# Attention heads of a gated-linear-attention layer cut into fifteen placed pieces

## The chip, the cores and the metric

The kernel runs on one core of a Trainium2 chip. The metric is the device time of one execution in microseconds (us). Engines are named as in the profile: PE is TensorE's matmul, PEld its weight load, DVE VectorE, ACT ScalarE, POOL GpSimd, SP the queue from which every DMA of this kernel is issued.

## The reference, cut to what matters

One decoder layer over 2048 tokens of width 1024: a gated-linear-attention mixer, then a gated feed-forward part with a causal convolution, each modulated by a conditioning vector, each with a layer normalisation after it.

```python
def gla_mixer(h, w_in, w_a2, b_a, norm_g, w_o):       # 4 heads, key width 128, value width 256, chunks of 64
    q, k, v, r, a_lr = jnp.split(h @ w_in, [...], axis=-1)
    log_a = jax.nn.log_sigmoid((a_lr @ w_a2 + b_a)) / 16.0
    bcum = jnp.cumsum(chunks(log_a, GLA_DK), axis=3)
    q_dec, k_inv, k_dec = qf * exp(bcum), kf * exp(-bcum), kf * exp(blast - bcum)
    att = where(causal, q_dec @ k_inv.T, 0);  o_intra = att @ vf
    def step(state, xs):                               # over the chunks
        o = q_dec @ state
        state = state * exp(blast)[..., None] + k_dec.T @ v
    o = (o_intra + o_inter) * rsqrt(mean(o * o) + 1e-5) * norm_g
    return (o * silu(r)) @ w_o

def conv_ffn(h, w_up, conv_w, conv_b, w_down): ...     # (silu(conv(u)) * g) @ w_down

x = layer_norm(alpha * x + (1 + gate) * mixer(x * (1 + scale) + shift))   # and the same with conv_ffn
```

## The kernel before

Every float32 product is made of three float32r products: an operand is split into a high half (a cast on ACT, L105) and a low half (a subtraction on DVE, L108), and `mm3` issues high x high, high x low, low x high (L111 to L113).

The tokens are four blocks (`tb` 0 to 3) of 512. First come the projections of block 0 and of `v` and `r` for all blocks, the latter by seven products for a 2x2 block product (`v_group`, `r_group`). Four products `X[0]`, `X[4]`, `X[2]`, `X[1]` of operands also serve the rank-16 gate rows: block 1's first half is `X[0]` plus the difference `X[4]`, so `gate_rows` multiplies both with `waw` and adds them in PSUM. `decays` makes the decay factors of a head from such rows: a product, then ACT and DVE in turn (L582 to L597).

Then comes the attention stage, in *units*. It goes through seven segments, `Q1 Q2 O0 Q3 O1 O2 O3`: a Q segment makes queries and keys of a block, an O segment multiplies a block's gated heads with `w_o`. A segment has eight units of 24 matmuls of 128x512 into four banks `ps_mm`; after four units the banks are emptied (`qk_out` by ACT, L667 and L668; `zs`, the residual sum, by DVE, L1375). `tick()` between units calls what a table puts there. `at_unit(u, fn)` enters a step; in the version before, a step's place is rounded down to a whole unit.

A head is a chain of such steps, `head_l` (loads of `E` and `qk`), `head_s` (decayed queries `Q`, keys `KI` and `KK`, on DVE), `head_a` (transposes of `KK`, L1208, and two groups of scores `Q,KI`, masked into `attm`, L1223 and L1224), `head_v` and `head_r` (loads), `head_b` (products `v,KTt` that update the state `S`, L1254, whose split halves `Shl` are made at once), `head_c` (outputs `v,at` and `Shl,Q`, copied to `on`, L1276) and `head_d` (two transposes of `on`, L1290, gated into `sr`, L1292). All of these and the transposes of the normalised rows (`ln1_out`, L1327) use four small banks `ps_w` in turn. `H_AT`, `STEP`, `LN_AT` and the other tables hold the places.

What the tables give is the order in which the code is recorded. A scheduler then orders each engine's instructions by priority and estimated readiness; `tc.high_priority(offset=...)` moves a few forward. All DMAs are issued by SP in one order, and each engine executes its instructions in its order. Weights and operands arrive in four buffers `raw`, and the split halves of two units are made ahead.

```python
STEP = (-1, 0, 2, 2, 3, 4, 5, 7)   # units after H_AT: head_l, _s, _a, _v, _b, _r, _c, _d
```

Of the kernel before, what the change touches and what calls it, by code (L numbers as in the profile page):

```python
# [17 lines left out]
P = 128  # L18
D = 1024
S = 2048  # L20
# [19 lines left out]
def kernel(  # L40
# [164 lines left out]
    a3_d = [dram.tile([96, TB], F32, name=f"a3_d{t}") for t in range(NTB)]  # L205
    xm1_d = [[dram.tile([P, 1024], F32, name=f"xm1_d{t}_{r}") for r in range(4)] for t in range(NTB)]
# [174 lines left out]
    def at_unit(u, fn, *a):  # L381
        steps.setdefault(math.floor(u), []).append((u, fn, a))

    def tick():
        u = pos[0]
        pos[0] += 1
        for _, fn, a in sorted(steps.pop(u, []), key=lambda s: s[0]):
            fn(*a)
# [39 lines left out]
    if True:  # L428
# [139 lines left out]
        def decays(tb, heads):  # L568
# [7 lines left out]
            for h in heads:  # L576
# [26 lines left out]
        def mm_a(pa, w, xs, kts):  # L603
            for kt in kts:
                for n, xm in enumerate(xs[kt]):
                    end = kt == KT - 1 and n == len(xs[kt]) - 1
                    nc.tensor.matmul(pa[0:96], w[:, kt], xm[0], start=kt == 0 and n == 0, stop=False)
                    nc.tensor.matmul(pa[0:96], w[:, kt], xm[1], start=False, stop=end)
# [7 lines left out]

        def waw_load():
# [22 lines left out]
        def s_part(banks, u, xm, lo_last=False):  # L640
# [9 lines left out]
            for n in range(4):  # L650
                for k in range(2):
                    kt = 2 * u + k
                    mm3(banks[n], (wv[:, 0, n, k], wv[:, 1, n, k]), xm[kt],
                        kt == 0, kt == KT - 1)

# [8 lines left out]
        def qk_out(tb, h, pq, pk):  # L664
            t = raw_tile("qk")
            with tc.high_priority(offset=0):
                nc.scalar.copy(t[:, 0:512], pq)  # L667
                nc.scalar.copy(t[:, 512:1024], pk)  # L668
            store(qk_d[tb][h], t)
            made.add(("qk", tb, h))  # L670
# [4 lines left out]
        def gemm_start():  # L675
# [51 lines left out]
            for pr in range(4):  # L727
# [35 lines left out]
                mm_a(pa, waw, {kt: [xm[kt]] for kt in kts}, kts)  # L763
# [10 lines left out]
            evac_a(pa, 0)  # L774
# [67 lines left out]
        def v_group(hf, X):  # L842
# [7 lines left out]
            for i in PROD:  # L850
# [22 lines left out]
                for t in range(4):  # L873
                    if i in (0, 5, 6):
                        dst = {0: p1, 5: u2, 6: u3}[i][t]
                        with tc.high_priority(offset=600):
                            nc.scalar.copy(dst, A[t])
# [184 lines left out]
        R_AT = ((8, 11, 12), (43, 45, 46))  # L1062
# [3 lines left out]
        WAW_AT = (11, 44, 52)  # L1066
        for u in WAW_AT:
            at_unit(u, waw_load)
        GR_AT = (17, 49, 56)
# [12 lines left out]
        M_AT = (36, 37.5, 38, 39, 40, 41, 42, 43, 51, 52, 53, 54, 55, 56, 57, 58)  # L1082
        MF_AT = (50, 49, 56, 61)
# [4 lines left out]
        at_unit(63, mod2)  # L1088
        at_unit(GR_AT[1], gate_rows, 2, XN1)
        at_unit(GR_AT[2], gate_rows, 3, XN1)  # L1090
        G_AT = (54, 55, 56, 57, 58, 59, 60, 61, 62)
# [54 lines left out]
        assert pos[0] == B0, pos  # L1146
        evx.close()
# [8 lines left out]
        Shl = [None] * NH  # L1156
# [37 lines left out]
        def head_v(H):  # L1194
            H["v"] = []
            for s in range(4):
                v = ab.tile([P, 2, DV], F32R, tag="v", name="v", bufs=7)
# [7 lines left out]
        def head_a(H):  # L1205
# [3 lines left out]
            KTt = zp.tile([P, 2, 512], F32R, tag="z", name="KTt")  # L1209
            with tc.high_priority(offset=60):  # L1210
                split(KTt[:, 0], KTt[:, 1], pt)
            H["KT"] = KTt
            KI, Q = H["KI"], H["Q"]
            H["at"] = []
            for g in range(2):
                pa = psum("w", 4)
                pav = pa[:, 0:384].rearrange("p (s c) -> p s c", s=2)
                for i in range(2):
                    s = 2 * g + i
                    tk = slice(s * P, s * P + P)  # L1220
                    mm3(pav[:, i], (KI[:, 0, tk], KI[:, 1, tk]), (Q[:, 0, s], Q[:, 1, s]), True, True)
                am = attm[g]
# [3 lines left out]
                at = ab.tile([P, 2, 2, P], F32R, tag="at", name="at", bufs=4)  # L1226
                split(at[:, 0], at[:, 1], am)
                H["at"].append(at)

        def head_b(H):  # L1230
            h, v, KTt, el = H["h"], H["v"], H["KT"], H["el"]
            H["S"] = []
            for g in range(2):
                pst = psum("w", 4)
                for i in range(2):
                    s = 2 * g + i
                    H["S"].append(Shl[h])
                    if H["last"] and s == 3:
                        continue
                    tk = slice(s * P, s * P + P)  # L1240
                    po = pst[:, i * DV:i * DV + DV]
                    mm3(po, (KTt[:, 0, tk], KTt[:, 1, tk]), (v[s][:, 0], v[s][:, 1]), True, True)
                for i in range(2):
                    s = 2 * g + i
                    if H["last"] and s == 3:
                        continue
                    po = pst[:, i * DV:i * DV + DV]
                    old = S32[:, h] if i == 0 else new
                    new = S32[:, h] if i == 1 else t2p.tile([P, DV], F32, tag="t2", name="S1")
                    with tc.high_priority(offset=0):  # L1250
                        if H["S"][s] is None:
                            nc.vector.tensor_copy(new, po)
                        else:
                            nc.vector.scalar_tensor_tensor(new, old, el[:, 1, s:s + 1], po, op0=ALU.mult, op1=ALU.add)  # L1254
                    st1 = ab.tile([P, 2, DV], F32R, tag="Shl", name="Shl", bufs=8)
                    split(st1[:, 0], st1[:, 1], new)
                    Shl[h] = st1
                    if i == 0:
                        H["S"][-1] = st1

        def head_c(H):
            h, v, Q = H["h"], H["v"], H["Q"]
            on = zp.tile([P, 4, DV], F32, tag="z", name="on")
            ss = smp.tile([P, 4], F32, tag="ss", name="ss")
            for g in range(2):
                po = psum("w", 4)
                at = H["at"][g]
                for i in range(2):
                    s = 2 * g + i
                    pos_ = po[:, i * DV:i * DV + DV]  # L1270
                    st = H["S"][s]
                    mm3(pos_, (at[:, 0, i], at[:, 1, i]), (v[s][:, 0], v[s][:, 1]), True, st is None)
                    if st is not None:
                        mm3(pos_, (Q[:, 0, s, 0:128], Q[:, 1, s, 0:128]), (st[:, 0], st[:, 1]), False, True)
                with tc.high_priority(offset=0):
                    nc.scalar.copy(on[:, 2 * g:2 * g + 2].rearrange("p s c -> p (s c)"), po)  # L1276
# [6 lines left out]
            H["on"] = on  # L1283

        def head_d(H):
            on, sr = H["on"], H["sr"]
            for e in range(2):
                pt = psum("w", 4)
                for s in range(4):
                    nc.tensor.transpose(pt[:, s * P:s * P + P], on[:, s, e * P:e * P + P], ident)  # L1290
                with tc.high_priority(offset=1200):
                    nc.vector.scalar_tensor_tensor(sr[:, e], pt, ng_sb[:, e:e + 1], sr[:, e], op0=ALU.mult, op1=ALU.mult)  # L1292
# [22 lines left out]

        def ln1_out(tb, zs, prs, by_act=False):
            for pr in prs:
                if zs is None:
                    z = z_tile("zc")
                    for t in range(4):  # L1320
                        load(z[:, t * 256:t * 256 + 256], zn_d[tb * 4 + t][:, pr * 256:pr * 256 + 256])
                for k in range(2):
                    kt = 2 * pr + k
                    pt = psum("w", 4)
                    for t in range(4):
                        src = z[:, t * 256 + k * P:t * 256 + k * P + P] if zs is None else zs[t][:, kt * P:kt * P + P]
                        nc.tensor.transpose(pt[:, t * P:t * P + P], src, ident)  # L1327
                    xt = t2p.tile([P, TB], F32, tag="t2", name="xt")
                    if by_act:
                        nc.scalar.activation(xt, pt, AF.Identity, bias=B2[:, kt:kt + 1], scale=A2[:, kt:kt + 1])  # L1330
                    else:
                        nc.vector.tensor_scalar(xt, pt, A2[:, kt:kt + 1], B2[:, kt:kt + 1], op0=ALU.mult, op1=ALU.add)
# [562 lines left out]
```

## Time and profile before

| | |
|---|---|
| median of 3 runs | 2153.97 us (2152.64 to 2156.61) |
| profiled execution, its own time | 2154.09 us |
| its span, first to last instruction | 2151.4 us |
| PE, DVE, ACT, POOL busy | 2103.0, 1565.6, 1042.9, 109.6 us |
| mean granted clock | 0.992 |

A row of the timeline has the start in us, the duration, engine, line, operation, output and inputs by the program's names, the shape, and in brackets how long the engine stood before it and who released it. Matmuls are pipelined: the duration of one is longer than the distance between two starts.

### The profile page before, as it was taken

How to read it: one execution, taken by the hardware profiler on the slowest of the kernel's cores; microseconds unless marked ns; L12 is line 12 of the kernel's file. 1: busy time of each engine (PE TensorE's matmuls, PEld its weight loads, DVE VectorE, ACT ScalarE, POOL GpSimd, SP SyncE). 2: the span in 40 equal slices, each digit the busy share in tenths (PEclk: the TensorE clock that was granted, in tenths of full speed). 3: DMA queues.
4: the chain of work that ended last, by engine and by line, in shares of the span. 5: the costliest groups of instructions: out<-in, count | busy, mean ns of one | idle time of the engine just before them, and what ended most of it. 6: DMA issues, size and time to landing. Idle time of an engine off the chain costs nothing.

```text
span 2151.4 us, 27162 instructions
## 1 busy us (share of the span) xinstructions
PE 2103.0 (98%) x9741; PEld 1747.5 (81%) x9741; DVE 1565.6 (73%) x2143; ACT 1042.9 (48%) x1523; POOL 109.6 (5%) x250
## 2 busy tenths in 40 slices
PE   9999999999989989999999999999999999999998
PEld 8887788788878868788888888888888888888887
DVE  6856767677876865987878788766666797578557
ACT  4648746665566643554444444333333443344332
POOL 0000000001020111000000000000000000021001
PEclk9999999999999999999999999999999999999999
DMA  9777988878958877677946669877777797677662
GB/s 366 278 262 290 316 293 308 306 275 287 323 198 310 311 277 289 242 271 269 327 175 216 211 231 327 309 253 266 262 255 268 273 334 273 193 239 253 195 204 89
DMA packets 199063, 571.52 MB, mean 266 GB/s; under 512 B 25008, under 2 KB 41776, under 8 KB 189200
## 3 DMA queue, kind: packets, MB, share of 16 engines
q1 hardware_dynamic: 198928, 569.80, 75.1%
q8 instruction: 76, 1.25, 0.2%
q14 instruction: 59, 0.48, 0.1%
HBM read 379.01 MB, written 190.71 MB: 265 GB/s over the span
## 4 chain that ended last, share of the span: by engine, by line
PE 82%; DVE 5%; DMA 5%; ACT 5%; issue 2%; POOL 1%; SPq 0%; DVEq 0%; ACTq 0%; POOLq 0%
PE ps_mm L111 18%; PE ps_mm L113 18%; PE ps_mm L112 18%; PE ps_w L111 8%; PE ps_w L112 8%; PE ps_w L113 8%; DMA raw<-in_wab_dram 1%; ACT hl L105 1%; DMA mraw<-in_mws_dram 1%; PE ps_mm L491 1%; PE ps_w L750 1%; PE ps_w L1327 1%; DVE xc L108 1%; DMA qk<-qk_d 1%; DMA v<-v_d 0%
## 5 line engine op out<-in xcount | busy, mean ns | idle before, releaser
L111 PE MATMUL ps_mm<-xc,hl 128*128 128x512 f32 x856 | 335.7, 392 | 6.0 <-ACT u L422 4.3
L112 PE MATMUL ps_mm<-xc,hl 128*128 128x512 f32 x856 | 334.0, 390 | 0.0
L113 PE MATMUL ps_mm<-xc,hl 128*128 128x512 f32 x856 | 333.2, 390 | 0.1
L111 PEld LDWEIGHTS ps_mm<-xc,hl 128*128 128x128 f32 x856 | 161.1, 188 | 42.0 <-ACT u L422 5.7
L113 PEld LDWEIGHTS ps_mm<-xc,hl 128*128 128x128 f32 x856 | 161.0, 188 | 34.2 <-DVE hl L108 0.7
L112 PEld LDWEIGHTS ps_mm<-xc,hl 128*128 128x128 f32 x856 | 161.2, 188 | 33.6 <-issue 0.5
L111 PE MATMUL ps_w<-xc,hl 128*128 128x512 f32 x432 | 168.4, 390 | 1.1 <-ACT hl L105 1.0
L113 PE MATMUL ps_w<-xc,hl 128*128 128x512 f32 x432 | 168.2, 389 | 0.3 <-DVE hl L108 0.3
L112 PE MATMUL ps_w<-xc,hl 128*128 128x512 f32 x432 | 168.1, 389 | 0.0
L1492 DVE SCALAR_TENSOR_TENSOR ct<-U,cw_sb,ct 128x512 f32<-128x512 f32 x176 | 131.8, 749 | 25.1 <-ACT ct L1486 22.6
L105 ACT CAST dhl<-raw 128x1024 fp32r<-128x1024 f32 x57 | 60.0, 1053 | 159.9 <-PE ps_mm L113 96.7
L422 ACT COPY u<-ps_mm 128x512 f32<-128x512 f32 x104 | 60.8, 584 | 158.2 <-PE ps_mm L113 153.4
L105 ACT CAST hl<-raw 128x1024 fp32r<-128x1024 f32 (+1 forms) x87 | 85.2, 981 | 102.8 <-PE ps_mm L113 39.8
L108 DVE TENSOR_TENSOR hl<-raw,hl 128x1024 fp32r<-128x1024 f32 (+1 forms) x87 | 98.6, 1136 | 49.9 <-ACT hl L105 49.4
L105 ACT CAST hl<-wu 128x1024 fp32r<-128x1024 f32 x82 | 86.3, 1053 | 94.6 <-PE ps_mm L113 68.0
L108 DVE TENSOR_TENSOR hl<-wu,hl 128x1024 fp32r<-128x1024 f32 x82 | 100.3, 1223 | 32.1 <-ACT hl L105 31.5
L108 DVE TENSOR_TENSOR dhl<-raw,dhl 128x1024 fp32r<-128x1024 f32 x57 | 69.7, 1223 | 66.5 <-ACT dhl L105 66.5
L111 PE MATMUL ps_mm<-hl,xg 128*128 128x512 f32 x256 | 102.8, 402 | 6.3 <-DVE zs L1375 4.2
L111 PE MATMUL ps_mm<-dhl 128*128 128x512 f32 x264 | 102.7, 389 | 0.0
L112 PE MATMUL ps_mm<-dhl 128*128 128x512 f32 x264 | 102.7, 389 | 0.0
L113 PE MATMUL ps_mm<-dhl 128*128 128x512 f32 x264 | 102.7, 389 | 0.0
L113 PE MATMUL ps_mm<-hl,xg 128*128 128x512 f32 x256 | 101.6, 397 | 0.0
(297 smaller groups left out, 5106.7 us busy)
## 6 DMA issues: line engine op xcount, KB each, us to landing
hc_d<-ct SPq DMA_DIRECT2D x154, 256.0 KB, 2.8
raw<-hc_d SPq DMA_DIRECT2D x70, 512.0 KB, 4.3
draw<-wc_d SPq DMA_DIRECT2D x70, 512.0 KB, 4.7
raw<-in_wab_dram SPq DMA_DIRECT2D x48, 512.0 KB, 6.4
hl<-wq_d SPq DMA_DIRECT2D x24, 1024.0 KB, 7.4
wu<-in_wup_dram SPq DMA_DIRECT2D x44, 512.0 KB, 5.3
wg<-in_wup_dram SPq DMA_DIRECT2D x44, 512.0 KB, 4.4
wh_d<-hl SPq DMA_DIRECT2D x22, 1024.0 KB, 4.8
```

What stands on the lines that cost most here:

```text
L105: accs["copy"] = nc.scalar.copy(h, src)
L108: return nc.vector.tensor_tensor(l, src if lsrc is None else lsrc, h.bitcast(F32), op=ALU.subtract)
L111: nc.tensor.matmul(po, a[0], b[0], start=first, stop=False, skip_group_check=resumed)
L112: nc.tensor.matmul(po, a[0], b[1], start=False, stop=False, skip_group_check=resumed)
L113: return nc.tensor.matmul(po, a[1], b[0], start=False, stop=last, skip_group_check=resumed)
L422: return t, nc.scalar.copy(t, po)
L491: mm = nc.tensor.matmul(pm[:, 256:512], still[:, 0:P], still, start=True, stop=True)
L750: nc.tensor.matmul(po, wv[:, a, kt], xm[kt][b], start=kt + a + b == 0, stop=kt == KT - 1 and b == 1)
L1327: nc.tensor.transpose(pt[:, t * P:t * P + P], src, ident)
L1492: nc.vector.scalar_tensor_tensor(ct, U[:, o + i:o + i + 512], cw_sb[:, j, i:i + 1], ct, op0=ALU.mult, op1=ALU.add)
```

## The change

The gate product of `X[0]` is kept: `keep_a` stores block 0's first half (and `X[0]`'s of the third block) to DRAM, `ak_back` loads it, and the second and fourth block multiply only `X[4]` and `X[2]` and add it on DVE. In `decays` the minimum and the subtraction are one instruction. In the attention stage a unit has four quarters of six matmuls with a step's place at each; a head's chain has fifteen pieces with places in quarters; PE's order there is the recorded one (`manual_schedule` for PE alone; the other engines are still ordered by the scheduler). The four banks of a segment are emptied one by one in the last unit, q and k into two tiles taken when the four units begin. State halves are split where they are used: the ones that a block inherits at its start (`head_i`), and not after the last update. There are eight `v` buffers for seven and seven `Shl` for eight. The transposes of normalised rows are placed one by one; six of them go to ACT instead of DVE; the second block's come one to 2.75 units after its segment, not three to four.

```diff
     def at_unit(u, fn, *a):
-        steps.setdefault(math.floor(u), []).append((u, fn, a))
+        steps.setdefault(u, []).append((fn, a))
...
+    def quarter(q):
+        with ExitStack() as behind:
+            if len(drained) > 99:
+                behind.enter_context(tc.issue_after(drained[-1 - 99].ins))
+            run_to(pos[0] - 0.75 + 0.25 * q)
+        pos[0] += q == 3
...
-                nc.vector.tensor_scalar(mn, mn, 0.0, None, op0=ALU.min)
...
-                nc.vector.tensor_tensor(mn, mn, az, op=ALU.subtract)
+                nc.vector.scalar_tensor_tensor(mn, mn, 0.0, az, op0=ALU.min, op1=ALU.subtract)
...
         def gate_rows(tb, X):
             w = accs.pop("waw")
+            pa = psum("w", 4)
             if tb == 2:
-                xs = [[X[0][k]] for k in range(4)] + [[X[1][k]] for k in range(4)]
+                mm_a(pa, w, X[0], range(4))
+                ak = keep_a(pa, 1)
+                pa = psum("w", 4)
+                mm_a(pa, w, [None] * 4 + X[1], range(4, KT))
             else:
-                xs = [[X[0][k], X[4][k]] for k in range(4)] + [[X[2][k]] for k in range(4)]
-            pa = psum("w", 4)
-            mm_a(pa, w, xs, range(KT))
-            evac_a(pa, tb)
+                ak = ak_back(tb // 2)
+                mm_a(pa, w, X[4] + X[2], range(KT))
+            add(nc.vector, ak, ak, pa[0:96])
+            evac_a(ak, tb)
...
+        def state(H):
+            st = ab.tile([P, 2, DV], F32R, tag="Shl", name="Shl", bufs=7)
+            split(st[:, 0], st[:, 1], H["new"])
+            H["S"].append(st)
...
+                with tc.high_priority(offset=1200):
...
+                        nc.vector.scalar_tensor_tensor(new, old, el[:, 1, s:s + 1], po, op0=ALU.mult, op1=ALU.add)
+                if s < 3:
+                    state(H)
...
         def q_segment(tb):
             for ps_ in range(2):
                 banks = [psum("mm", 4) for _ in range(4)]
+                outs = [raw_tile("qk") for _ in range(2)]
                 for u in range(4):
-                    s_part(banks, u, operand[key])
-                    if u < 3:
-                        tick()
-                for n in range(2):
-                    qk_out(tb, 2 * ps_ + n, banks[2 * n], banks[2 * n + 1])
-                tick()
+                    def done(n):
+                        if u == 3:
+                            with tc.high_priority(offset=300):
+                                i = nc.scalar.copy(outs[n // 2][:, n % 2 * 512:n % 2 * 512 + 512], banks[n])
+                            drained.append(i)
...
+                        quarter(n)
+                    s_part(banks, u, operand[key], done=done)
...
-        H_AT = (1, 3, 6, 9, 12, 14, 17, 20, 23, 25, 28, 31, 34, 36, 39, 42)
-        STEP = (-1, 0, 2, 2, 3, 4, 5, 7)
+        H_AT = (1, 3.75, 8.5, 9.25, 12, 14.75, 17.0, 20.25, 23, 25.75, 28.5, 31.0, 33.75, 36.5, 39.25, 42)
+        STEP = (-1, 0, 2, 2.25, 2.5, 2, 2.75, 3.25, 3.5, 4, 5.25, 5.5, 5.5, 7.5, 7.75)
...
-        for kind, tb in SEG:
-            (q_segment if kind == "Q" else o_segment)(tb)
+        with tc.manual_schedule(engines={getattr(mybir.EngineType, e) for e in ('PE',)}):
+            for kind, tb in SEG:
+                (q_segment if kind == "Q" else o_segment)(tb)
```

PE in segment O0 before, at the place where the first pieces of head 5 meet the last of head 3 (heads are counted from 0 over the four blocks; `on` are outputs of head 3, `KI32`, `Q` and `KI` belong to head 5, `ps_w` with a number is one use of a small bank, `ps_mm` one of a projection's banks; of each group of equal matmuls the first row is shown):

```order
L1290 MATMUL ps_w_4811<-ident_91,on_4599 128x128 x4
L1290 MATMUL ps_w_4817<-ident_91,on_4599 128x128 x4
L1208 MATMUL ps_w_4825<-ident_91,KI32_4688 128x128 x4
L111 MATMUL ps_w_4833<-Q_4685,KI_4690 128x192
...
L111 MATMUL ps_w_4845<-Q_4685,KI_4690 128x192
...
L111 MATMUL ps_mm_4779<-hl_4711,xg_4565 128x512
```

The same engine and place in the changed program (its `mm3` stands one line higher, the transposes are L1326 and L1242):

```order
L1326 MATMUL ps_w_4827<-ident_91,on_4622 128x128 x4
L1242 MATMUL ps_w_4833<-ident_91,KI32_4693 128x128 x4
L110 MATMUL ps_mm_4721<-hl_4591,xg_4497 128x512
...
L1326 MATMUL ps_w_4855<-ident_91,on_4622 128x128 x4
L110 MATMUL ps_w_4861<-Q_4690,KI_4695 128x192
...
L110 MATMUL ps_mm_4718<-hl_4722,xg_4818 128x512
...
L110 MATMUL ps_w_4908<-v_4580,at_4611 128x256
...
L110 MATMUL ps_w_4922<-Q_4690,KI_4695 128x192
```

Before, five uses of the four banks follow each other with no projection between them; now six projection matmuls stand after every one or two uses.

ACT at the end of the second four units of Q1, before (the four copies empty the projection's banks):

```order
L105 CAST Shl_3997<-S32_3540 128x256
L667 COPY qk_4051<-ps_mm_3751 128x512
L668 COPY qk_4051<-ps_mm_3752 128x512
L667 COPY qk_4055<-ps_mm_3753 128x512
L668 COPY qk_4055<-ps_mm_3754 128x512
L105 CAST xg_4061<-xraw_4062 128x1024
```

And now:

```order
L1401 COPY qk_3711<-ps_mm_3707 128x512
L1311 COPY on_3927<-ps_w_3929 128x512
L1317 ACTIVATE sq_3974,ss_3928<-on_3927 128x256 x2
L104 CAST at_3949<-attm1_3532 128x256
L1401 COPY qk_3711<-ps_mm_3708 128x512
L1311 COPY on_3927<-ps_w_3960 128x512
```

Each bank's copy now stands apart from the next one's, with work of the heads between them.

More of the change, by code (lines that the diff above doesn't have):

```diff
@@ L205 @@
     a3_d = [dram.tile([96, TB], F32, name=f"a3_d{t}") for t in range(NTB)]
+    ak_d = [dram.tile([96, TB], F32, name=f"ak_d{t}") for t in range(2)]
     xm1_d = [[dram.tile([P, 1024], F32, name=f"xm1_d{t}_{r}") for r in range(4)] for t in range(NTB)]
@@ L601, in decays, with mm_a @@
                 made.add(("E", tb, h))
-        def mm_a(pa, w, xs, kts):
+        def mm_a(pa, w, xs, kts, first=True, last=True):
             for kt in kts:
[L605 to L608, printed above, removed]
+                nc.tensor.matmul(pa[0:96], w[:, kt], xs[kt][0], start=first and kt == kts[0], stop=False)
+                nc.tensor.matmul(pa[0:96], w[:, kt], xs[kt][1], start=False, stop=last and kt == kts[-1])
         def evac_a(pa, tb):
@@ L615, in evac_a, with keep_a, ak_back @@
             made.add(("a", tb))
+        def keep_a(pa, hf):
+            t = t2p.tile([96, TB], F32, tag="t2", name="ak")
+            nc.scalar.copy(t, pa[0:96])
+            store(ak_d[hf], t)
+            made.add(("ak", hf))
+            return t
+        def ak_back(hf):
+            assert ("ak", hf) in made
+            t = t2p.tile([96, TB], F32, tag="t2", name="ak")
+            load(t, ak_d[hf])
+            return t
         def waw_load():
@@ L654, in s_part @@
                         kt == 0, kt == KT - 1)
+                if done is not None:
+                    done(n)
         def gemm_f(xm, tag):
@@ L1225, in head_a @@
                                           pav[64:128, :, 128:192])
[L1226 to L1230, printed above, removed]
-            h, v, KTt, el = H["h"], H["v"], H["KT"], H["el"]
[L1232 to L1259, printed above, removed]
@@ L1261, in head_c @@
-        def head_c(H):
-            h, v, Q = H["h"], H["v"], H["Q"]
[L1263 to L1276, printed above, removed]
+            at = ab.tile([P, 2, 2, P], F32R, tag="at", name="at", bufs=4)
@@ new lines, in head_c @@
+        def head_c(H, g):
+            h, v, Q = H["h"], H["v"], H["Q"]
+            if g == 0:
+                H["on"] = zp.tile([P, 4, DV], F32, tag="z", name="on")
+                H["ss"] = smp.tile([P, 4], F32, tag="ss", name="ss")
+            on = H["on"]
+            po = psum("w", 4)
+            at = H["at"][g]
+            for i in range(2):
+                s = 2 * g + i
+                pos_ = po[:, i * DV:i * DV + DV]
+                st = H["S"][s]
+                mm3(pos_, (at[:, 0, i], at[:, 1, i]), (v[s][:, 0], v[s][:, 1]), True, st is None)
+                if st is not None:
+                    mm3(pos_, (Q[:, 0, s, 0:128], Q[:, 1, s, 0:128]), (st[:, 0], st[:, 1]), False, True)
+            with tc.high_priority(offset=0):
+                nc.scalar.copy(on[:, 2 * g:2 * g + 2].rearrange("p s c -> p (s c)"), po)
@@ L1282, in head_c, with head_d @@
                 nc.scalar.activation(on[:, s], on[:, s], AF.Copy, scale=ss[:, s:s + 1])
-            H["on"] = on
-        def head_d(H):
+        def head_d(H, e):
             on, sr = H["on"], H["sr"]
[L1287 to L1292, printed above, removed]
+            pt = psum("w", 4)
+            for s in range(4):
+                nc.tensor.transpose(pt[:, s * P:s * P + P], on[:, s, e * P:e * P + P], ident)
+            with tc.high_priority(offset=0):
+                nc.vector.scalar_tensor_tensor(sr[:, e], pt, ng_sb[:, e:e + 1], sr[:, e], op0=ALU.mult, op1=ALU.mult)
+            if e == 0:
+                return
             made.add(("g", H["tb"], H["h"]))
@@ L1403, in x_first @@
             up, X0 = late_up["up"], late_up["X0"]
[L1404 removed]
+            assert all(("x", b, 2 * p + k) in made for b in range(2) for p in (pr, 2 + pr) for k in range(2))
             tiles = {i: x_tile(up, i) for i in (0, 4, 5, 1)}
```

182 lines of the change are left out of this document (112 added, 70 removed).

## Prediction

> **What bounds the kernel now.** I read the page's first part, then the stages, then the waits of TensorE (PE), and last the timeline around the longest of them.
>
> ```profile
> PE 2103.0 (98%) x9741; PEld 1747.5 (81%) x9741; DVE 1565.6 (73%) x2143; ACT 1042.9 (48%) x1523; POOL 109.6 (5%) x250
> ```
>
> PE is busy for 98% of the span, so only two things are worth time: matmuls that go away, and the 48 us in which PE stands. The stretches show where these are (columns: stretch, length, then busy us and instructions of PE, PEld, DVE, ACT, POOL, then the granted clock, DMA share, GB/s).
>
> ```profile
> 0.00:432.00 432.00, 421.88 (x1885) 344.14 (x1886) 303.44 (x377) 264.13 (x345) 2.11 (x14) 0.99 0.83 302
> 432.00:918.00 486.00, 455.50 (x2441) 388.93 (x2440) 362.86 (x604) 279.43 (x542) 56.55 (x119) 0.98 0.77 279
> 918.00:2106.00 1188.00, 1188.00 (x5255) 983.56 (x5254) 862.81 (x1100) 487.23 (x620) 40.77 (x101) 1.00 0.74 254
> 2106.00:2151.00 45.00, 37.64 (x167) 30.83 (x165) 36.51 (x63) 12.07 (x19) 10.21 (x16) 0.95 0.25 94
> ```
>
> The feed-forward part (918 to 2106) has no idle PE at all: whatever the change moves there is worth nothing. The attention stage (432 to 918) has 30.5 us of idle PE, and that is where the heads are placed anew. Its waits, as PE sees them:
>
> ```profile
> PE ps_w L111 <- DVE sr L1292: 6.0, 2, 5.5
> PE ps_w L111 <- ACT on L1276: 5.9, 3, 5.3
> PE ps_w L1327 <- DVE S L1254: 5.6, 1, 5.6
> PE ps_mm L111 <- DVE zs L1375: 4.2, 3, 2.1
> PE ps_mm L111 <- ACT qk L667: 2.2, 2, 1.4
> PE ps_w L111 <- DMA v<-v_d: 1.2, 1, 1.2
> PE ps_w L1327 <- DVE attm L1224: 1.0, 1, 1.0
> PE ps_w L111 <- DVE S L1254: 0.8, 1, 0.8
> PE ps_w L1208 <- DVE KI L1191: 0.7, 1, 0.7
> ```
>
> Columns: who waited for whom, us in total, times, longest. Two families: `ps_w` (the four small banks, which the pieces of the heads share) makes 6.0+5.9+5.6+1.2+1.0+0.8+0.7 = 21.2 us, of which three waits of about 5.5 are 16.4; `ps_mm` (the four banks of a projection) makes 6.4. The first long one in order of time:
>
> ```profile
> 527.56 0.42 SPq L1165 DMA_DIRECT2D qk<-qk_d  x1
> 531.72 1.03 PE L1290 MATMUL ps_w<-ident,on 128*128 128x128 f32 x8
> 532.59 0.60 PE L1208 MATMUL ps_w<-ident,KI 128*128 128x128 f32 x4
> 533.56 0.27 PE L113 MATMUL ps_w<-Q,KI 128*128 128x192 f32 x1
> 534.94 0.43 DVE L1178 SCALAR_TENSOR_TENSOR Q<-qk,E 128x256 f32<-128x256 f32 x1 [4.46 <-DMA qk<-qk_d]
> 537.35 1.23 DVE L133 TENSOR_TENSOR raw<-raw,G 128x1024 f32<-128x1024 f32 x1 [0.79 <-DMA raw<-in_wab_dram]
> 538.50 1.40 DVE L1292 SCALAR_TENSOR_TENSOR sr<-ps_w,ng_sb,sr 128x512 f32<-128x512 f32 x2
> 539.30 0.53 PE L111 MATMUL ps_w<-Q,KI 128*128 128x192 f32 x1 [5.46 <-DVE sr L1292]
> ```
>
> PE transposes a finished head into two banks at 531.72, goes on at once with the next head's transposes and scores, and needs the first of those banks again at 533.7. The DVE instruction that empties it runs at 538.50, because DVE stood for 4.46 us for the next head's `qk`. So a stall needs both: an eviction that comes late, and a PE order that wants the bank back within two microseconds.
>
> Behind such a stall the clock is low as well:
>
> ```profile
> 539.00:545.50 6.50, 6.20 (x18) 5.14 (x19) 6.40 (x11) 2.90 (x5) 0.00 (x0) 0.50 0.65 251
> 622.20:627.50 5.30, 5.09 (x15) 4.32 (x16) 5.25 (x10) 4.70 (x14) 1.04 (x3) 0.50 0.94 276
> 784.00:788.00 4.00, 4.00 (x14) 3.22 (x13) 4.00 (x8) 1.74 (x3) 0.00 (x0) 0.50 0.17 66
> ```
>
> At 0.50 half of the 6.2+5.1+4.0 = 15.3 us of PE time there is lost, 7.7 us. Idle and clock together, the stage can give back at most 21.2+6.4+7.7 = 35.3 us.
>
> **The change part by part.** The profiled execution took 2154.09 us with a span of 2151.4; it lies 0.12 above the median of the runs, so the sum serves for both.
>
> *Gate product stored.* It removes 16 matmuls of 96x512 on PE (24 become 16 for the second and the fourth block).
>
> ```profile
> 156.12 0.39 PE L607 MATMUL ps_w<-xc,waw 128*96 128x512 f32 x1
> 156.35 0.39 PE L608 MATMUL ps_w<-xc,waw 128*96 128x512 f32 x1
> 46.60 0.81 ACT L696 ACTIVATE xc<-xraw,md 128x512 fp32r<-128x512 f32 x1 [7.00 <-DVE md L265]
> 538.61 1.05 ACT L105 CAST hl<-raw 128x1024 fp32r<-128x1024 f32 x1 [8.03 <-DVE raw L133]
> 539.82 1.22 DVE L108 TENSOR_TENSOR hl<-raw,hl 128x1024 fp32r<-128x1024 f32 x1
> ```
>
> The duration 0.39 is not the price, the distance of two starts is: 0.23 us. 16 x 0.23 = **-3.7**, all of it on PE's path. It adds two ACT copies and four DVE additions of 96x512 (about 0.5 and 0.6 each, half of the 1.05 and 1.22 that the last two rows show for twice the width), two stores and three loads on SP. The first copy falls into the 7.00 us in which ACT stands before 46.60; the rest is read three and more units later, at the decays. Cost 0; without that cover 0.6 once.
>
> *Projection banks drained one by one* (q and o segments): the waits are 6.4 us. The last of the `zs` ones is a late load:
>
> ```profile
> 802.26 0.69 DVE L1375 SCALAR_TENSOR_TENSOR zs<-zs,ps_mm 128x512 f32<-128x512 f32 x1 [1.94 <-DMA zs<-in_x_dram]
> ```
>
> Those tiles come free when the second block's normalised transposes are done; these move 1.25 units forward, so the load starts earlier. Between 0 and 6.4; nearest to 6.4, since both reasons are removed: **-5**.
>
> *Fifteen placed pieces.* Counted from the two orders with the starts' distances, a small bank is wanted again less than 2 us of PE work after its last write 18 times of 166 before and never after; under 3 us 31 times against 5. At the stall above the distance grows from 1.7 to about 4 us, so if the eviction is as late as before, each of the three long waits still shrinks by about 2.5, and the small ones (4.8 us together) go: 12.3. If the lateness goes too, 21.2. I take **-14**, nearer the first, since nothing in this edit makes the `qk` load earlier except an eighth `v` buffer.
>
> *The clock behind the stalls*: 0 to -7.7. Three waits of 5.5 become about 2.9 each, and two rows show what such waits do:
>
> ```profile
> 253.93 1.20 PE L111 MATMUL ps_w<-hl,xc 128*128 128x512 f32 x4 [1.91 <-ACT hl L105]
> 255.80:259.00 3.20, 3.20 (x9) 2.48 (x8) 2.35 (x4) 1.67 (x2) 0.00 (x0) 0.50 0.78 234
> 803.00:807.00 4.00, 3.96 (x16) 2.94 (x17) 3.82 (x7) 0.58 (x3) 0.00 (x0) 1.00 0.82 318
> ```
>
> A wait of 1.91 was followed by half the clock, one of 2.08 (before 803.00) was not. So half: **-4**. The Trainium skill ("TensorE: Matmul & The Clock Gate", Part 1) says that the array falls to half its clock only after a whole idle window of about 3.4 us, and comes back after as long a busy one. By that rule every remaining wait would be free of it, the term -7.7 and the sum 3.7 us lower; the row at 253.93 is against the rule, the one at 803.00 agrees.
>
> *More changes between kinds of matmul on PE.* A lone group of four transposes inside a projection:
>
> ```profile
> 634.79 0.40 PE L112 MATMUL ps_mm<-xg,hl 128*128 128x512 f32 x1
> 635.16 0.66 PE L1327 MATMUL ps_w<-ident,zs 128*128 128x128 f32 x4
> 635.57 0.48 PE L113 MATMUL ps_mm<-xg,hl 128*128 128x512 f32 x1
> 635.89 0.40 PE L111 MATMUL ps_mm<-xg,hl 128*128 128x512 f32 x1
> ```
>
> From 635.02 (634.79 plus one distance) to 635.57, and 0.09 more until the next distance is normal: 0.64 us. Eight together took 531.72 to 532.59, 0.44 for four. The new order has 52 separate runs of transposes for 34: 18 x 0.2 = **+3.5**. Bounds: 0 if the gap before these rows is only a bank wait; 26 if each of the 131 additional changes of kind cost 0.2. I stay near the lower, since a row shows it for transposes alone.
>
> *Normalised transposes placed earlier.* In the second block PE reaches them one unit after the segment's end instead of three. The nearest rows are the waits of `L1327`, 1.0 and 5.6: between 0 and 5.6, **+2**.
>
> *One instruction for minimum and subtraction*: 16 DVE instructions fewer, in a chain whose waits DVE shares with evictions; PE does not read it directly. *State halves at use*: the same 60 pairs of casts and subtractions, later. *Six transposed outputs on ACT*, 48% busy. Together 0; their worth is inside the eviction terms.
>
> Sum: -3.7 -5 -14 -4 +3.5 +2 = -21.2, so 2154.1 - 21.2 = **2133 us**.
>
> **The rivals.**
>
> *All waits of the stage vanish.* For: no distance below 2 us is left. Against: DVE is at 363 of 486 us there, and its waits for DMA remain. -3.7-35.3+2 (some kind changes) = -37: **2117**.
>
> *The lateness is the cause, not the order.* DVE stands for loads that SP issued late (527.56, landed 7 us later), whatever PE does; then the long waits keep their length to within a microsecond, and only the gates, the projection banks and the small waits pay: -3.7-5-4.8+3.5+2 = -8: **2146**.
>
> *Slower: held raw tiles.* The q segments now take their two output tiles when a pass begins and hold them for four units, out of four buffers that also carry the weights.
>
> ```profile
> raw<-in_wab_dram SPq DMA_DIRECT2D x4, 512.0 KB, 7.2
> ```
>
> One turn of a buffer is 7.2 us of landing, 1.05 and 1.2 of the split (rows above), 9.5 us; two buffers give a tile every 4.7 us. A unit is about 8.1 us (455.5 us of busy PE over 56 units) and asks for one weight tile and half an operand tile, one every 5.4. Above that PE waits 1.5 times the difference in each of the 24 units of these segments. It decides against the change from 0.9 us a unit (21 us), when a landing takes 9.7 us; at 10.5 us it is 1.5 a unit, 36 us, -21+36 = +15: **2169**. Against: the two next tiles are already split ahead at each time.
>
> *It does not do what it says*: DVE and ACT are still ordered by the scheduler, which knew PE's old order just as well; new waits equal to the old appear: **2152**.
>
> **How the numbers follow.** What a measurement of this kernel can tell from no change is about 0.2%, 4.3 us: faster is below 2149.7, slower above 2158.3. Chances: my forecast (2122 to 2142) 0.50; all waits gone 0.18; lateness the cause 0.15; slower 0.10; no effect 0.07. Faster: 0.50+0.18+0.15 less 0.01 of the third = 0.82; same 0.08; slower 0.10. The range reaches from the second case with 3 us of error, 2114, to the third with 4, 2150; outside stay the last two, and some 0.03 below.
>
> **What the profile after would show.** Gates: 64 instead of 80 matmuls with `waw`. Pieces: no `ps_w` wait above 3 us in the stage and PE idle there about 11 us instead of 30; a wait above 5 speaks for the late loads, with DVE standing for `qk` before it. Banks: the waits of `ps_mm` on `qk` and `zs` below 2 us together. Clock: 1.00 in all stretches of the stage if the waits are short. Raw tiles: PE waits on `hl` with ACT standing for `raw` would show the slower case. I am wrong if the idle PE moves to the normalised transposes, or if the feed-forward part, where nothing was idle, has become slower.

## The result and the profile after

The changed kernel took 2138.16 us in the median of 4 runs (2136.79 to 2139.73), the kernel before 2153.45 us beside it: a ratio of 0.9927, 95% interval 0.9909 to 0.9944, or 15.3 us less. In a second comparison it was 0.9926 (0.9912 to 0.9941). The prediction was 2133 us (2114 to 2150). The profiled execution took 2139.29 us.

First the line of busy times, then stretches with the columns of those shown before: of the kernel before, the attention stage from the first Q matmul to the last O matmul; of the changed kernel the same stage, and the feed-forward part.

```profile
PE 2098.2 (98%) x9725; PEld 1740.5 (81%) x9725; DVE 1558.0 (73%) x2125; ACT 1046.0 (49%) x1529; POOL 110.7 (5%) x250
```
```profile
402.93:878.50 475.57, 446.57 (x2409) 382.37 (x2408) 343.39 (x578) 269.86 (x528) 54.05 (x116) 0.98 0.79 285
```
```profile
402.13:859.66 457.53, 442.18 (x2408) 376.83 (x2407) 333.20 (x560) 272.64 (x532) 54.35 (x116) 0.99 0.83 299
905.00:2092.00 1187.00, 1186.33 (x5247) 981.63 (x5246) 861.34 (x1099) 486.55 (x619) 41.37 (x100) 1.00 0.74 253
```

PE has the same matmuls in the stage (the 16 fewer of the page's first line are gate rows ahead of it; the two counts differ by one record). The stage is 18.0 us shorter: its idle PE falls from 29.0 to 15.4 us (length less busy), 13.6, and PE's busy time by 4.4 us, which is mostly clock. The terms of the prediction for this stage make 17.5. What PE still waits for in the whole execution, as far as it matters here (who, for whom, us in total, times, longest; the first row, for `u`, lies outside the stage, the third just behind it):

```profile
PE ps_mm L110 <- ACT u L437: 6.6, 4, 3.3
PE ps_mm L110 <- DVE zs L1427: 6.0, 5, 2.0
PE ps_mm L110 <- DVE z L1427: 2.8, 1, 2.8
PE ps_w L110 <- DVE sr L1328: 2.4, 2, 2.2
PE ps_w L110 <- DVE attm L1258: 1.8, 1, 1.8
PE ps_w L1367 <- ACT zs L1348: 1.4, 1, 1.4
PE ps_w L1367 <- DVE S L1291: 1.2, 1, 1.2
PE ps_w L110 <- ACT on L1311: 0.4, 1, 0.4
```

The three `ps_w` waits of 5.5 us are gone; the longest left is 2.2. The waits of the projection banks for `qk` are gone, those for `zs` are not. One line is new: `z`, the last block's residual sum, at the start of the feed-forward part. From the last O matmul to the first down-projection matmul PE now needs 845.05 us instead of 840.59, 4.5 more. The timeline of that place, DVE and PE, and then the stretch behind it:

```profile
861.18 0.50 PE L110 MATMUL ps_w<-xc,hl 128*128 128x512 f32 x1 [1.13 <-ACT hl L104]
862.20 1.22 DVE L107 TENSOR_TENSOR xc<-xs,xc 128x1024 fp32r<-128x1024 f32 x1
863.34 0.69 DVE L341 TENSOR_TENSOR wu<-wu 128x512 f32<-128x512 f32 x1
863.94 1.28 DVE L1427 SCALAR_TENSOR_TENSOR z<-z,ps_mm 128x512 f32<-128x512 f32 x2
864.68 0.80 PE L110 MATMUL ps_mm<-xc,hl 128*128 128x512 f32 x1 [2.76 <-DVE z L1427]
```
```profile
864.68:870.20 5.52, 5.52 (x13) 4.36 (x14) 5.52 (x7) 2.84 (x4) 0.20 (x2) 0.50 0.58 191
```

The last O matmul starts at 859.66, but the banks are emptied from 863.94 on: DVE first makes operands for the feed-forward part. PE stands 2.76 us and then runs at half the clock for 5.5 us. Behind it is one number that the prediction did not price: the evictions of `zs` and `z` went from priority 300 to 0. The heads' evictions changed their priorities too (transposed keys from 60 to 0, the state update from 0 to 1200, `sr` from 1200 to 0). None of these stands in the part of the diff shown above.

### The profile page after: what moved, and what is told of

It reads as the page before. It is cut to its first block, busy times and chain, and to the rows that moved or that the text cites. A ratio compares the mean times of both kernels' runs of the same rounds, so it can differ in the third digit from the quotient of the medians.

```text
span 2137.6 us, 27133 instructions
## 1 busy us (share of the span) xinstructions
PE 2098.2 (98%) x9725; PEld 1740.5 (81%) x9725; DVE 1558.0 (73%) x2125; ACT 1046.0 (49%) x1529; POOL 110.7 (5%) x250
## 3 DMA queue, kind: packets, MB, share of 16 engines
q8 instruction: 76, 1.25, 0.2%
## 4 chain that ended last, share of the span: by engine, by line
PE 61%; DVE 1%; DMA 1%; issue 0%; ACT 0%; DVEq 0%; SPq 0%; ACTq 0%
PE ps_mm L110 14%; PE ps_mm L112 14%; PE ps_mm L111 14%; PE ps_w L112 7%; PE ps_w L110 7%; PE ps_w L111 7%; DVE xs L341 0%; DVE xc L107 0%; PE ps_w L1367 0%; DMA xs<-xm_d 0%; DMA hc_d<-ct 0%; DMA raw<-hc_d 0%; PE ps_w L1326 0%; ACT dhl L104 0%; DVE ct L341 0%
```

## The experiments

Twelve kernels ran, each beside the kernel before; 0.001 of a ratio is 2.15 us.

| kernel | ratio | 95% interval | us against before |
|---|---|---|---|
| changed kernel, again | 0.9926 | 0.9912 to 0.9941 | -15.9 |
| gates_alone | 0.9992 | 0.9982 to 1.0003 | -1.7 |
| gates_left_out | 0.9978 | 0.9969 to 0.9987 | -4.7 |
| pieces_alone | 0.9958 | 0.9943 to 0.9972 | -9.0 |
| whole_units | 1.0046 | 1.0031 to 1.0062 | +9.9 |
| drain_at_end | 0.9920 | 0.9903 to 0.9937 | -17.2 |
| z_first | 0.9901 | 0.9884 to 0.9918 | -21.3 |
| new_order_old_priorities | 0.9918 | 0.9905 to 0.9932 | -17.6 |
| whole_units_old_priorities | 1.0075 | 1.0061 to 1.0089 | +16.1 |
| transposes_one_unit_later | 0.9944 | 0.9931 to 0.9957 | -12.1 |
| decays_one_unit_later | 0.9928 | 0.9915 to 0.9941 | -15.5 |
| two_instructions | 0.9904 | 0.9888 to 0.9920 | -20.7 |

**The priority of z.**

```diff
# z_first, against the changed kernel
-                            with tc.high_priority(offset=0):
+                            with tc.high_priority(offset=300):
                                 i = nc.vector.scalar_tensor_tensor(zs[t][:, cs_], ...)
```

> The changed kernel with the o segments' evictions (the zs and z instructions on DVE) at the priority that they had before (300 instead of 0); one number changes. If their low priority is what costs 4.5 us between the last projection and the first down-projection matmul, and what keeps 6.0 us of ps_mm waits for zs: 2138.2 less 4.5 to 9, 2129 to 2134 us, with no wait above 1 us on z at the start of the feed-forward part. If those evictions only change places with others that PE needs as soon (sr, KTt, x_first): 2136 to 2140 us, and the ps_w waits grow by what the ps_mm waits lose.

The changed kernel was run again beside other variants:

> The changed kernel once more, on the chip of these runs, as the measure for the variants of it: 15 us below the kernel before; and 5 to 6 us above z_first if the priority of the z evictions costs what the first comparison showed. The first gate rows start between 25 and 28 us in either kernel if their start is chance.

It was 15.9 below, and its first gate row starts at 25.23 us, where it started at 27.95 in the first profile and at 25.15 in the kernel before: that start is chance. The changed kernel's two ratios less that of z_first are 0.0026 and 0.0025, some 5.5 us (the intervals just overlap, but no run of z_first took longer than the fastest of the changed kernel's nine); z_first is the fastest version of this study, 2129.0 us. The same place in its timeline, where the last O matmul starts at 850.55:

```profile
850.50 1.28 DVE L1427 SCALAR_TENSOR_TENSOR z<-z,ps_mm 128x512 f32<-128x512 f32 x2
851.33 0.47 PE L110 MATMUL ps_mm<-xc,hl 128*128 128x512 f32 x1 [0.39 <-DVE z L1427]
```

The wait is 0.39 instead of 2.76 us, and the matmul behind it takes 0.47, not 0.80. PE's waits for `zs` fall to 2.8 us. This is the first theory, near the lower end of what it gave.

Where the 5.5 us lie is not where the stall suggested. The stage of z_first, and two waits of PE behind the place of the stall:

```profile
398.60:850.55 451.95, 440.79 (x2408) 373.76 (x2407) 333.14 (x561) 272.48 (x532) 55.90 (x116) 1.00 0.84 302
```
```profile
858.12 0.50 PE L110 MATMUL ps_mm<-xc,hl 128*128 128x512 f32 x1 [1.06 <-ACT hl L104]
884.48 0.50 PE L110 MATMUL ps_mm<-xc,h 128*128 128x512 f32 x1 [1.34 <-ACT u L437]
```

The stage is 5.6 us shorter than in the changed kernel's first profile and 7.7 shorter than in its second. From the last O matmul to the first down-projection matmul z_first still takes 843.21 us, 1.8 and 0.8 less than those two profiles (845.05 and 843.96) and 2.6 more than before: PE now waits there for other operands.

**Draining the banks.**

```diff
# drain_at_end, against the changed kernel (q segment; the o segment in the same way, at priority 300)
-                                i = nc.scalar.copy(outs[n // 2][...], banks[n])
+                            if n == 3:
+                                with tc.high_priority(offset=0):
+                                    for m in range(4):
+                                        nc.scalar.copy(outs[m // 2][...], banks[m])
```

> The changed kernel with the four banks of a projection drained together after the last one, with the priorities of the kernel before. By the prediction's term: 5 us more, 2143 us, with ps_mm waits for qk and zs near 6.4 + 6 us. By the trace of the changed kernel, where the waits for zs are still 6.0 us and only those for qk (2.2) are gone: 2 us more, 2140 us.

Neither: 1.3 us less than the changed kernel, inside the uncertainty. Its waits are 2.5 for `zs`, 0.7 for `z` and none for `qk`, although all four banks are emptied at the end as before. But this kernel differs from the changed one in two things, the emptying and the priority of `zs` and `z`. With the priority set right in both, z_first against this kernel, emptying one by one is worth 4 us. The two intervals overlap, so this is not shown, but it is near the -5 of the prediction: four of z_first's five runs are below all six of this kernel.

**The order of the pieces.**

```diff
# whole_units, against the changed kernel
-        H_AT = (1, 3.75, 8.5, 9.25, 12, 14.75, 17.0, 20.25, ...)
-        STEP = (-1, 0, 2, 2.25, 2.5, 2, 2.75, 3.25, 3.5, 4, 5.25, 5.5, 5.5, 7.5, 7.75)
+        H_AT = (1, 3, 8, 9, 12, 14, 17, 20, ...)
+        STEP = (-1, 0, 2, 2, 2, 2, 2, 3, 3, 4, 5, 5, 5, 7, 7)
```

> The changed kernel with the heads' pieces put on whole units again (offsets rounded down; still fifteen pieces, drained banks, stored gate product). In PE's order a small bank is then wanted again less than 2 us after its last write 9 times of 166 (before: 18, changed kernel: 0) and under 3 us 21 times (31 and 5). If the order on PE carries the gain of the attention stage: half to two thirds of the 14 us come back, less some 2 us of fewer changes between kinds: 2143 to 2148 us, with PE's ps_w waits of the stage between 12 and 20 us. If the gain comes from the other engines' new order (evictions earlier whatever PE does): within 2 us of the changed kernel, 2136 to 2140 us, and ps_w waits as there.

Worse than either theory: 26 us slower than the changed kernel, 10 slower than before. Its stage takes 483.34 us, 25.8 longer than the changed kernel's, with these waits and this granted clock:

```profile
PE ps_w L1367 <- ACT zs L1348: 8.4, 3, 6.4
PE ps_w L1367 <- DVE attm L1258: 4.7, 2, 3.3
PE ps_w L110 <- DVE sr L1328: 4.6, 3, 2.3
PE ps_w L1242 <- DVE KI L1225: 3.7, 1, 3.7
```
```profile
404.85:888.19 483.34, 451.78 (x2408) 385.26 (x2407) 331.95 (x561) 273.52 (x533) 58.58 (x116) 0.96 0.78 283
```

Not all of this is small banks wanted back early. The longest wait, 6.4 us, is one of the transposes of normalised rows for the rows themselves (`zs`, made by ACT), and the wait for `KI` is for data too. By the count in the expectation this order has half as many early reuses as the kernel before (9 for 18), and yet its stage is 7.8 us longer than before (483.34 for 475.57). So a bunched order costs time in more ways than by early reuse of a bank.

Whether low priorities had made it so bad, the next two asked, with one edit on z_first, and the tables of whole_units on top of that:

```diff
# new_order_old_priorities, against z_first: heads' evictions as before (keys 60, state 0, sr 1200)
-            with tc.high_priority(offset=0):
+            with tc.high_priority(offset=60):
                 split(KTt[:, 0], KTt[:, 1], pt)
...
-                with tc.high_priority(offset=1200):
+                with tc.high_priority(offset=0):
                     if H["S"][s] is None:
...
-            with tc.high_priority(offset=0):
+            with tc.high_priority(offset=1200):
                 nc.vector.scalar_tensor_tensor(sr[:, e], pt, ...)
# whole_units_old_priorities: H_AT and STEP of whole_units as well
```

> z_first, and the other evictions of the heads too at the priorities of the kernel before (transposed keys 60 instead of 0, state update 0 instead of 1200, gated output sr 1200 instead of 0). If a spread order leaves time enough for each eviction, their rank on DVE matters little: within 3 us of z_first, 20 to 26 us below the kernel before. If the new priorities of the heads are part of the gain, as the low priority of z was part of a loss: 5 us or more slower than z_first.

> The same priorities as new_order_old_priorities, and the pieces on whole units; with it and whole_units it makes a table of order by priorities. If the order on PE is worth the time by itself: 12 to 20 us slower than new_order_old_priorities, with ps_w waits of 15 us or more in the stage. If whole_units lost its 23 us because evictions of low priority met an order that wants the banks at once: within 6 us of new_order_old_priorities.

With the spread order the priorities of the heads are worth 3.7 us, between the two cases foretold; the intervals overlap, so it is not told from zero. With the bunched order the kernel is 34 us slower than with the spread one. So the order on PE carries the gain under either set of priorities. (Bunched pieces with the new places of the other tables are worse than the kernel before, so 26 and 34 us are not the gain over before.)

DVE's waits for the heads' `qk` loads, the lateness of the prediction's third case, say the same. Before, in the changed kernel, in new_order_old_priorities and in whole_units they are:

```profile
DVE Q L1178 <- DMA qk<-qk_d: 9.4, 5, 4.5
DVE Q L1212 <- DMA qk<-qk_d: 9.9, 6, 3.0
DVE Q L1212 <- DMA qk<-qk_d: 9.4, 5, 4.3
DVE Q L1212 <- DMA qk<-qk_d: 2.9, 3, 2.0
```

DVE stands for these loads as long as before in the second and third, which have no `ps_w` wait above 2.2 us, and least in the fourth, which has the most. So the long `ps_w` waits do not follow the lateness.

The spread pieces by themselves:

```diff
# pieces_alone, against the changed kernel
-                mm_a(pa, w, X[4] + X[2], range(KT))      # and the 24 gate matmuls as before
+                xs = [[X[0][k], X[4][k]] for k in range(4)] + [[X[2][k]] for k in range(4)]
...              # banks as in drain_at_end, minimum and subtraction apart
-        LT_AT = (..., (40, 40.25, 40.5, 40.75, 41.25, 41.25, 41.5, 41.75), ...)
+        LT_AT = (..., (41, 41.25, 41.5, 41.75, 42.25, 42.25, 42.5, 42.75), ...)
```

> The fifteen placed pieces with the new order on PE, without the rest: 24 gate matmuls again in the second and fourth block, the banks of a projection drained together with the old priorities, the second block's normalised transposes one unit later, minimum and subtraction as two instructions. By the prediction's terms: pieces -14, clock -4, changes of kind +3.5: 14.5 below the kernel before. By the runs so far (changed kernel -15.3; gates -1 to -2, draining together about 0 with the old priority of z, earlier transposes -9): -7 to -11, with the wait for zs of 6.4 us in the sixth segment still there.

9.0 us less (6.0 to 12.3), as the runs before it gave and 5.5 short of the prediction's terms. (The kernel also keeps the other tables' new places, the heads' new priorities, the later state halves, the eighth `v` buffer and the six outputs on ACT, and its normalised transposes are still a quarter to one unit earlier than before.) Its profiled execution is the fastest of its five (2141.47 us); there the stage takes 461.0 us, 14.6 less than before, and the way from the stage's end to the first down-projection matmul 2.4 more. Even in that stage a gain is given back: where PE waited 2.08 us for `zs` before (the last such wait of the page's 4.2), it now waits 6.96. SP's loads before, then the loads, the eviction and PE in pieces_alone:

```profile
794.63 1.90 SPq L1342 DMA_DIRECT2D zs<-in_x_dram  x4
```
```profile
773.94 1.88 SPq L1370 DMA_DIRECT2D zs<-in_x_dram  x4
779.14 0.69 DVE L1412 SCALAR_TENSOR_TENSOR zs<-zs,ps_mm 128x512 f32<-128x512 f32 x1 [1.17 <-DMA zs<-in_x_dram]
779.88 0.80 PE L110 MATMUL ps_mm<-hl,xg 128*128 128x512 f32 x1 [6.96 <-DVE zs L1412]
```

With the heads' stalls gone PE comes to these banks 28 us earlier (at 772.92, where it came to the second of them at 800.92), and the loads that their eviction needs go out only 20.7 us earlier.

**The normalised transposes.** On z_first the second block's were moved back by one unit, the last line of the diff above.

> z_first with the normalised transposes of the second block one unit later. The prediction's term for their earlier place is +2: if so, 2 us less, with no wait at these transposes (1.2 and 1.1 in z_first). If their place pays by freeing the tiles for the next block's loads (the bank term): 2 to 5 us more, with ps_mm waits for zs back behind a DMA wait of DVE.

9.3 us slower than z_first, more than the rival gave. The chain in this kernel (PE's last such transpose, SP's loads of the next block's rows, DVE's eviction, PE's wait for a bank), and then in z_first:

```profile
772.18 0.60 PE L1367 MATMUL ps_w<-ident,zs 128*128 128x128 f32 x4
774.51 1.85 SPq L1388 DMA_DIRECT2D zs<-in_x_dram  x4
779.80 0.69 DVE L1427 SCALAR_TENSOR_TENSOR zs<-zs,ps_mm 128x512 f32<-128x512 f32 x1 [1.31 <-DMA zs<-in_x_dram]
780.55 0.80 PE L110 MATMUL ps_mm<-hl,xg 128*128 128x512 f32 x1 [6.38 <-DVE zs L1427]
```
```profile
758.16 0.60 PE L1367 MATMUL ps_w<-ident,zs 128*128 128x128 f32 x4
760.50 2.60 SPq L1388 DMA_DIRECT2D zs<-in_x_dram  x4
767.56 0.69 DVE L1427 SCALAR_TENSOR_TENSOR zs<-zs,ps_mm 128x512 f32<-128x512 f32 x1 [2.23 <-DMA zs<-in_x_dram]
771.51 0.50 PE L110 MATMUL ps_mm<-hl,xg 128*128 128x512 f32 x1 [0.17 <-DVE zs L1427]
```

The four loads go out 2.3 us after the last transpose in both, and the first eviction starts 5.3 and 7.1 us after them. In z_first PE comes to the bank when that is over; a unit later it stands for nearly the whole of it.

**The stored gate product.** gates_alone is the kernel before with `keep_a`, `ak_back` and the shorter `gate_rows`; gates_left_out enlarges the term.

> The kernel before with the stored partial gate product alone (64 instead of 80 matmuls with waw; the rest as before). If PE's path sets these stretches, as the prediction had it: 16 x 0.23 = 3.7 us less, 2149.8 us. If ACT sets the second block's stretch (its decay chain with its table loads ends at the same time, and PE only comes to it earlier and waits), the 8 matmuls of the second block are worth nothing and the 8 of the fourth block count: 1.8 less, 2151.6 us, with a longer wait of PE for ACT near 213 us in the trace.

```diff
# gates_left_out, against the kernel before
+                nc.tensor.matmul(pa[0:96], w[:, 0], X[0][0][0], start=True, stop=False)
+                nc.tensor.matmul(pa[0:96], w[:, 4], X[2][0][1], start=False, stop=True)
+                evac_a(pa, tb)
+                return
```

> The kernel before, in which the gate rows of the second and fourth block are made with 2 matmuls instead of 24 each; 44 matmuls of 96x512 are left out (part of the computation is missing, so this is only a price). It enlarges the gate term, which 16 matmuls left too small to tell from the spread. If PE's path sets both places: 44 x 0.23 = 10.1 us below the kernel before. If ACT's chain sets the second block's stretch: only the fourth block's 22 count, 5.1 us.

The first lies beside 1.8 and, by its interval, can't exclude 3.7. The second decides: 4.7 (2.8 to 6.7) and not 10.1, so about half. The holder that this case names, ACT, is not what the trace of gates_left_out shows. SP's issue of the load of the gate rows `A` and PE's wait for it:

```profile
202.24 0.71 SPq L566 DMA_DIRECT2D A<-a_d  x1
208.89 0.79 PE L578 MATMUL ps_w<-A,w2s 96*128 96x512 f32 x1 [5.49 <-DMA A<-a_d]
```

In the kernel before SP issues that load at 202.20, with 22 more matmuls ahead of it on PE. The load does not move with PE, so what PE saves there it waits. In the changed kernel PE's wait there is for ACT (`u`, 3.26 us at 212.92). In gates_alone it is for ACT too, as foretold: 2.67 us for `u` at 211.01, where the kernel before has 1.32 at 214.07. So a load and ACT's `u` come ready there near the same time, and which of them PE waits for changes with the number of matmuls left out.

What the wait for ACT is worth, one kernel tried:

```diff
# decays_one_unit_later, against z_first
-        D_AT = (17, 20, 24, 27, 51, 54, 58, 62)
+        D_AT = (18, 20, 24, 27, 51, 54, 58, 62)
```

> z_first with the second block's first decays one unit later (18 instead of 17), after which ACT no longer changes its table twice inside one head's chain (30 table loads in the kernel for 33). If ACT's chain with its table loads holds PE near 212 us (3.3 us of wait for u, 2.8 lost to the low clock behind it): 4 to 6 us less than z_first, first Q matmul 4 to 6 us earlier from the first gate rows. If ACT is simply full there and the wait moves on: within 1.5 us of z_first.

A miss: it is 5.8 us slower than z_first by the ratios (their intervals just overlap), not 4 to 6 faster. The wait of 3.2 us at 211 went, and others came: 3.08 for `hl` at 202.50 and 3.48 for `u` at 217.06. What sets this stretch is open; from the first gate row to the first Q matmul the profiles of the variants that share its program lie between 372.0 and 378.0 us (this kernel: 377.7), so one profile can't place a term of 4 us there.

**One instruction for minimum and subtraction.**

```diff
# two_instructions, against z_first
+                nc.vector.tensor_scalar(mn, mn, 0.0, None, op0=ALU.min)
...
-                nc.vector.scalar_tensor_tensor(mn, mn, 0.0, az, op0=ALU.min, op1=ALU.subtract)
+                nc.vector.tensor_tensor(mn, mn, az, op=ALU.subtract)
```

> z_first with the decay minimum and subtraction as two instructions again (16 more on DVE). By the prediction 0: within 2 us of z_first (22.8 us below the kernel before). If DVE's 16 x 0.3 to 0.4 us lie in front of evictions that PE waits for: 3 to 6 us slower than z_first.

0.6 us slower than z_first: 0, as predicted.

## Why the prediction was right, step by step

The forecast case happened: the time is 5 us above the 2133 and inside the range. The mechanism was right for the heads' stalls; the sum came out near through errors of both signs, which is in part luck.

- **Pieces, clock behind the stalls, changes of kind: -14, -4, +3.5, together -14.5.** Measured alone -9.0 (6.0 to 12.3 less). The mechanism was right: three waits of 5.5 us became none above 2.3, by the order, while DVE stood for the `qk` loads nearly as long as before (8.2 us for 9.4). The step that failed is that the terms were added as if independent: 4.9 us (6.96 less 2.08) went into the wait for `zs`, and the way from the stage's end to the first down-projection matmul is 2.4 longer. In the whole change another of its parts, the earlier transposes, gives the first back.
- **Changes of kind, +3.5: too high.** A lone group of transposes in the changed kernel:

```profile
635.79 0.40 PE L112 MATMUL ps_mm<-xg,hl 128*128 128x512 f32 x1
636.03 0.60 PE L1367 MATMUL ps_w<-ident,zs 128*128 128x128 f32 x4
636.38 0.48 PE L110 MATMUL ps_mm<-xg,hl 128*128 128x512 f32 x1
636.69 0.40 PE L111 MATMUL ps_mm<-xg,hl 128*128 128x512 f32 x1
```

  0.35 from start to start and 0.08 more until the next distance is 0.23 again: 0.43, the same as 0.44 in a group of eight. The row that the prediction took (0.64) was no typical one; one lone group of the kernel before stood for all. Counted in the two traces, the stage has 60 separate runs of transposes for 36, not 52 for 34, but at no price for a split the term is 0 either way.
- **Banks drained one by one, -5, and normalised transposes earlier, +2.** Their sum of -3 is too small. What draining one by one is worth stays open: drain_at_end, which has the old priority of `z` too, is 1.3 us below the changed kernel; against z_first, with the same priority in both, it is -4, with overlapping intervals. The transposes are where the mistake is: one unit of their earlier place is -9.3, not +2. The prediction had the mechanism ("these move 1.25 units forward, so the load starts earlier") and booked it under the banks, and took the transposes' own term from waits of the old order, which are now 1.4 and 1.2.
- **Gates, -3.7:** -1.7, by the enlarged test about half. "All of it on PE's path" failed: no stall stood there, but a load, and in the changed kernel ACT, are ready there at their own time.
- **The priority of z: not in the sum.** +5.5, of which 0.8 to 1.8 at the start of the feed-forward part, by the profiles, and most of the rest in the stage.
- **Costed at nothing:** the decays' instruction, 0 in the runs. The later state halves were not tried alone.

Measured terms together: -9.0 - 9.3 - 1.7 + 5.5 + 0 = -14.5, beside the -15.3 and -15.9 of the whole. With the 4 us of the draining it is -18.6. The terms were measured in different kernels, so that they add up is not shown, and the sum is not good to better than 3 or 4 us.

Of what the profile after was to show: no `ps_w` wait above 3 us, right. Idle PE in the stage 11 us: 15.4. `qk` and `zs` below 2 us together: wrong, 6.0. Clock 1.00 throughout: not so behind two waits in the stage, of 1.80 and 2.16 us, where it was 0.69 over the next 5.5 us, 1.7 us lost behind each. The rival of held raw tiles: no wait for `hl` in the q segments shows. The rival of lateness: against it stand the `qk` waits of DVE, 9.4 before and 9.9 now, with the long `ps_w` waits gone. "I am wrong if the feed-forward part has become slower": it did, by 4.5 us, all of it at its start. With the priority set right 2.6 of these remain, and 2.4 in pieces_alone: that belongs to the new order or the other tables, and which of them is open.

## What to carry to other kernels

When stalls on shared PSUM banks go, ask what the engine then reaches sooner: a load tied to a buffer's release came 21 us earlier where the engine came 28 us earlier, and 5 us turned into a wait for it until the transposes that free the buffer were moved too. To tell a late load from an order that asks too early, compare the other engine's wait for the load before and after: here it stayed, and the stalls went. An eviction's priority is part of an edit's price, in the stage as well as at its end, where the next stage's work stands ready to go ahead of it; a stall that is easy to see there need not be where the time goes. And a matmul saved where PE is busy is worth its time only if what comes next doesn't arrive at a time of its own.

## What the runs showed of the hardware

After the same wait of the same instruction the clock did three things. PE's matmul behind the wait for `u` at 211 us and the 5.5 us after it, in z_first, in the second run of the changed kernel, and in drain_at_end:

```profile
211.05 0.50 PE L110 MATMUL ps_mm<-xc,hl 128*128 128x512 f32 x1 [3.23 <-ACT u L437]
211.05:216.60 5.55, 5.55 (x24) 4.61 (x25) 1.36 (x2) 5.47 (x6) 0.00 (x0) 1.00 0.94 349
```
```profile
210.53 0.50 PE L110 MATMUL ps_mm<-xc,hl 128*128 128x512 f32 x1 [3.23 <-ACT u L437]
210.53:216.00 5.47, 5.47 (x17) 4.34 (x18) 1.36 (x2) 5.39 (x6) 0.00 (x0) 0.69 0.98 350
```
```profile
210.14 0.79 PE L110 MATMUL ps_mm<-xc,hl 128*128 128x512 f32 x1 [3.23 <-ACT u L437]
210.14:215.70 5.56, 5.56 (x13) 4.40 (x14) 1.36 (x2) 5.49 (x6) 0.00 (x0) 0.50 0.94 341
```

In 5.5 us PE issues 24, 17 or 13 matmuls. By these rows 0.69 over 5.47 us would be 3.4 us at half the clock (0.31 x 5.47 / 0.5), a loss of 1.7 us. Counted from the distances of starts over all fourteen traces, without the first 30 us, 0.8 us or more were lost behind 7 of 87 waits of 1 to 1.5 us, 22 of 44 of 1.5 to 2.5, and 35 of 40 above 2.5 (the same wait often recurs from variant to variant, so these are fewer cases than they seem). So the clock's price of a wait is a chance that grows with its length; the prediction's half was the right size for waits near 2 us. The Trainium skill ("TensorE: Matmul & The Clock Gate", Part 1) asks for a whole idle window of about 3.4 us; the waits here that were shorter and still cost the clock are against that.
